# The first stage of a hybrid decoder layer: loads in quarters, three token tiles side by side, nine tiles on eight banks

## The chip, the cores and the metric

The kernel runs on one core of a Trainium2 chip, as one program. Its time is the device time of the whole program in microseconds (us); where several runs are shown, their median counts.

## The reference

The reference computes one layer of a hybrid decoder for two groups of requests: 1024 prompt tokens and 8 x 4 = 32 sample tokens of width 1024, all in fp32. Only the beginning of the layer is touched here. What matters of it:

```python
# u, v, cq, ckv, kpe: columns of one projection
u, v, cq, ckv, kpe = split_in(rms_norm(x, g_mix) @ w_in)    # widths 512, 512, 256, 256, 32

def chunk_gmlp(u, v, w_s, b_s, ln_g, ln_b):
    ...
    vg = layer_norm(gelu(v).reshape(n, t // c, c, 8, 64), ln_g, ln_b)
    w = where(tril(ones((c, c))), w_s[:, :c, :c], 0)
    mixed = einsum('gts,nmsgd->nmtgd', w, vg) + b_s[:, :c].T[:, :, None]
    return gelu(u) * mixed.reshape(n, t, 512), vg
```

Behind this come the latent attention over the prompt and over a paged cache, the output projection, attention into 256 memory tokens, and a gated convolutional FFN. They take most of the time and aren't changed.

## The kernel before

**Tiles.** The 1056 tokens are nine token tiles (`TILES`): eight of 128 (0 to 7, the prompt) and tile 8 of 32 (the samples). For the loads of x they are grouped into three chunks (`CH`) of 384, 384 and 288 tokens, so that a chunk covers three tiles. The 1024 features lie in eight blocks of 128 (k).

**Split products.** Each fp32 operand is written as a sum of two reduced-precision parts. `split` (L188) makes the high part on ACT (L192 a plain cast, L196 with a gain) and the low part on DVE (L193 or L199), and `mm3` (L180, matmul at L186) multiplies high by high, high by low and low by high. A tile of a projection, over eight blocks, is thus 24 matmuls into one PSUM bank. x is split once, into `xh` and `xl`, with the gain `g_mix` in it.

**The factor of the norm.** The RMS factor of a token is not put into x but applied afterwards: `rs_tok`, a scale for each token. `squares` (L315) has ACT square the token rows (L323, tiles `xt` for tokens 0 to 383 and space in `a_all` for the others) with a sum along the row, and DVE then makes the reciprocal root by some twelve small steps (`rsqrt`, L221 to L232). The gelu that reads a projection's bank (L426 for v, L456 for u) needs the `rs_tok` of its tile.

**Order of phase 1.** The columns of v and u come in two halves (`hf`), in this order: v0, u0, the gate products of half 0, v1, u1, the gate products of half 1. For each tile of v: 24 matmuls (`proj`, L342), the gelu (L426), and a LayerNorm over groups of 64 columns: sums on DVE (L427 to L432), squares on ACT (L431), the factor on DVE (L437), gain and bias on POOL (L439, L441). The result is split again into `vgh` (ACT) and `vgl` (DVE). The LayerNorm works on tiles 0 to 2, 3 to 5, 6 and 7, and 8 as groups. The gate products (`mm<-vgh,wsh`) need all eight tiles of `vgh` and `vgl`, and the matrices that `gate_matrices` (L370) makes; DVE takes them up at L467.

**Weights.** `wraw` loads a half's weights in two DMAs of four blocks, `wsplit` (L293) splits them in two steps of four blocks. There are two buffers each for raw and split weights.

**Banks.** The pool `ps1` has five PSUM banks named "mm", for all projections and gate products, and three named "st" for small sums.

**What sets the order.** Within phase 1 the SP queue, which issues the loads, follows the order in which the code is written until `loads.__exit__` (a manual schedule). Before the change that order is: v0's first half and x's chunk 0 first half, the same for the second halves, tokens of tile 0, chunk 1 in two halves, tokens of tiles 1 and 2, chunk 2, then tokens of tiles 3 to 6 (into `a_all`, in space that the loads of x free), the weights u0, the LayerNorm's rows, v1, and the matrices of the gate. The other engines' orders come from a scheduler that places instructions by its own estimates; a change in one place can reorder an engine elsewhere. Each engine then works its own list in order.

Of the kernel before, what the change touches and what calls it, by code (L numbers as in the profile page):

```python
# [5 lines left out]
F32 = mybir.dt.float32  # L6
# [7 lines left out]
P = 128  # L14
# [6 lines left out]
TILES = [(i * P, P) for i in range(8)] + [(NP_, NS)]  # L21
# [134 lines left out]
class Net:  # L156
# [122 lines left out]
    def phase1(self):  # L279
        nc, tc, I, O = self.nc, self.tc, self.I, self.O  # L280
        p = self.open("p1")
        pp = self.open("ps1", space=PSUM)
# [9 lines left out]

        def wsplit(name):  # L293
            raw = raws.pop(name)
            n = raw.shape[2]
            hi = self.t(p, [P, 8, 288], FR, "whi", 2)[:, :, :n]
            lo = self.t(p, [P, 8, 288], FR, "wlo", 2)[:, :, :n]
            for k in range(0, 8, 4):
                self.split(hi[:, k : k + 4], lo[:, k : k + 4], raw[:, k : k + 4])
            return hi, lo  # L300

        px = self.open("px")
        xts, xrs = [], []

        def xload(c, e):
            o, n = CH[c]
            xrs.append(self.t(px, [P, 4, 384], F32, "xr", 6)[:, :, :n])
            nc.sync.dma_start(xrs[-1], I["xT"][:, 4 * e : 4 * e + 4, o : o + n])

        def tload(i, place):  # L310
            t0, tn = TILES[i]
            xts.append(place[:tn])
            nc.sync.dma_start(xts[-1], I["x"][t0 : t0 + tn])

        def squares(p, i0, i1):  # L315
# [8 lines left out]
            self.rsqrt(p, self.rs_tok[:, i0:i1], ss, 1.0 / 1024)  # L324

        xt = lambda: self.t(px, [P, 1024], F32, "xt", 3)
        loads = tc.manual_schedule(engines={mybir.EngineType.SP})
        loads.__enter__()
        raws["v0"] = raw = self.t(pr, [P, 8, 288], F32, "wraw", 2)[:, :, :256]
        for e in range(2):  # L330
            k = slice(4 * e, 4 * e + 4)
            nc.sync.dma_start(raw[:, k], I["w_v0"][:, k])
            xload(0, e)
        tload(0, xt())
        for e in range(2):
            xload(1, e)
        tload(1, xt())
        tload(2, xt())
        for e in range(2):
            xload(2, e)  # L340
        w = wsplit("v0")
        for c, (o, n) in enumerate(CH):  # L342
            for k in range(8):
                self.split(xh[:, k, o : o + n], xl[:, k, o : o + n], xrs[2 * c + k // 4][:, k % 4], self.col("g_mix", k))
            if c == 0:
                squares(px, 0, 1)
            elif c == 1:
                squares(px, 1, 3)
        def proj(w, i, n):
            t0, tn = TILES[i]  # L350
            ps = self.t(pp, [P, 512], F32, "mm", 5)[:tn, :n]
            self.mm3(ps, [(xh[:, k, t0 : t0 + tn], xl[:, k, t0 : t0 + tn]) for k in range(8)],
                     [(w[0][:, k], w[1][:, k]) for k in range(8)])
            return ps
# [6 lines left out]
        for i in range(3, 7):  # L361
            tload(i, flat[:, (i - 3) * 1024 : (i - 2) * 1024])
        wraw("u0", I["w_u0"], 256)
        pg = self.open("pg")
# [37 lines left out]
        for hf in range(2):  # L402
# [8 lines left out]
            for i0, i1 in ((0, 3), (3, 6), (6, 8), (8, 9)):  # L411
# [9 lines left out]
                mu = self.t(pg, [P, 3, 4], F32, "mu", 2)[:tn, :m]  # L421
                rv = self.t(pg, [P, 3, 4], F32, "rv", 2)[:tn, :m]
                for i in range(i0, i1):
                    ps = proj(w, i, 256)
                    g, mi = gv[:, i - i0], mu[:, i - i0]
# [9 lines left out]
                for i in range(i0, i1):  # L435
# [1833 lines left out]
```

## Time and profile before

| quantity | value |
| --- | --- |
| median of 3 runs | 1914.36 us (1913.44 to 1916.24) |
| profiled execution | 1912.54 us |
| its span, first to last instruction | 1910.8 us |
| mean granted TensorE clock | 0.987 |
| PE busy | 1841.0 us (96%), 14338 matmuls |
| DVE busy | 1417.4 us (74%) |
| ACT busy | 929.5 us (49%) |
| POOL busy | 707.7 us (37%) |

The span is what the views of the trace divide; the 1.7 us between it and the execution's time lie around it. Times in the views are counted from the span's start. A row of a timeline has start, duration, engine, line, operation, output<-inputs, shapes and count, and in brackets the idle time before it and what released it. Matmuls overlap their successors, so the step from one start to the next, not the duration, tells the rate.

### The profile page before, as it was taken

To read this page: it belongs to the slowest core of one execution; us is meant where nothing else is said; L and a number is where in the kernel's file an instruction comes from. 1 tells how busy PE (TensorE), PEld (TensorE's weight loads), DVE (VectorE), ACT (ScalarE), POOL (GpSimd) and SP (SyncE) were. 2 spreads that over 40 slices of the span, in tenths; PEclk is the share of its full clock that TensorE was granted. 3 is DMA by queue.
4 is the path that set the end of the run, shared out by engine and by line. 5 is a ranking of instruction groups with operands and counts; after the bars stand their busy time and mean duration, and the time that the engine had idled before them with its cause. 6 is when DMAs were issued, how large, how long until landed. Compare 5 with 4: busy or idle time off the path is not lost.

```text
span 1910.8 us, 39909 instructions
## 1 busy us (share of the span) xinstructions
PE 1841.0 (96%) x14338; PEld 1724.7 (90%) x14338; DVE 1417.4 (74%) x3093; ACT 929.5 (49%) x1964; POOL 707.7 (37%) x816
## 2 busy tenths in 40 slices
PE   6999899999999999999899999999999999999999
PEld 6999777778989888989799988899999999999999
DVE  7865868776877677776754666688898888879664
ACT  6435676666555555555553355543333233345442
POOL 1221415643544454434313101057767667500000
PEclk9999899999999999999999999999999999999999
DMA  8102204656766655554564334422222322395242
GB/s 296 54 14 71 72 1 155 231 220 178 213 189 172 176 168 173 168 158 139 177 182 142 139 116 154 149 68 73 73 90 68 100 68 77 89 361 170 78 151 75
DMA packets 135704, 260.21 MB, mean 136 GB/s; under 512 B 20561, under 2 KB 78770, under 8 KB 132434
## 3 DMA queue, kind: packets, MB, share of 16 engines
q1 hardware_dynamic: 134642, 256.61, 42.8%
q8 instruction: 113, 1.85, 0.4%
q10 hardware_dynamic: 864, 1.05, 0.2%
q14 instruction: 85, 0.70, 0.1%
HBM read 212.30 MB, written 45.30 MB: 135 GB/s over the span
## 4 chain that ended last, share of the span: by engine, by line
PE 69%; DVE 9%; issue 5%; DMA 3%; POOL 2%; ACT 1%; SPq 0%; DVEq 0%; POOLq 0%; ACTq 0%
PE s L186 15%; PE d L186 12%; PE X L186 7%; PE b L186 7%; PE F L186 7%; PE E L186 6%; PE A L186 3%; PE y L186 2%; PE o L918 2%; PE tp L905 1%; PE o L1348 1%; DVE mx L1299 1%; POOL S L1296 1%; PE tp L860 1%; PE tp L186 1%
## 5 line engine op out<-in xcount | busy, mean ns | idle before, releaser
L186 PE MATMUL s<-w2h,ch 128*128 128x288 f32 (+1 forms) x1024 | 305.9, 299 | 0.0
L186 PE MATMUL s<-w2h,cl 128*128 128x288 f32 (+1 forms) x1024 | 295.1, 288 | 1.9 <-POOL cl L1235 1.9
L186 PE MATMUL s<-w2l,ch 128*128 128x288 f32 (+1 forms) x1024 | 294.6, 288 | 0.0
L186 PEld LDWEIGHTS s<-w2h,ch 128*128 128x128 f32 x1024 | 192.6, 188 | 19.1 <-issue 13.6
L186 PEld LDWEIGHTS s<-w2h,cl 128*128 128x128 f32 x1024 | 192.4, 188 | 2.4 <-POOL cl L1235 2.2
L186 PEld LDWEIGHTS s<-w2l,ch 128*128 128x128 f32 x1024 | 192.8, 188 | 0.0
L1278 DVE TENSOR_REDUCE ss<-sq 128x16 f32<-128x1024 f32 x128 | 155.4, 1214 | 47.8 <-ACT sq L1275 47.5
L1235 POOL TENSOR_TENSOR cl<-cT,ch 128x512 fp32r<-128x512 f32 x64 | 83.4, 1303 | 166.7 <-ACT ch L1231 154.3
L1275 ACT ACTIVATE sq<-s 128x512 f32<-128x512 f32 x128 | 76.5, 597 | 91.0 <-PE s L186 90.9
L1272 ACT ACTIVATE sq<-s 128x512 f32<-128x512 f32 x128 | 76.5, 598 | 82.1 <-PE s L186 81.7
L192 ACT CAST a<-brb 128x528 fp32r<-128x528 f32 x77 | 48.8, 634 | 110.7 <-PE d L186 107.3
L186 PE MATMUL mm<-whi,xh 128*128 128x256 f32 (+3 forms) x288 | 83.8, 292 | 16.1 <-ACT xh L196 9.9
L186 PE MATMUL d<-a,w 128*128 128x264 f32 x768 | 95.4, 284 | 1.2 <-DVE G L2048 1.2
L186 PEld LDWEIGHTS d<-a,w 128*128 128x128 f32 x768 | 94.3, 188 | 1.3 <-issue 1.3
L193 DVE TENSOR_TENSOR a<-brb,a 128x528 fp32r<-128x528 f32 x77 | 54.2, 705 | 55.5 <-ACT a L192 55.5
L186 PE MATMUL mm<-wlo,xh 128*128 128x256 f32 (+3 forms) x288 | 82.4, 289 | 0.0
L186 PE MATMUL mm<-whi,xl 128*128 128x256 f32 (+3 forms) x288 | 82.3, 290 | 0.0
L1925 POOL TENSOR_TENSOR lo<-s,hi 128x1024 fp32r<-128x1024 f32 x20 | 63.2, 3160 | 45.7 <-ACT hi L1924 45.7
L1974 ACT COPY a<-A 128x264 f32<-128x264 f32 x44 | 16.4, 374 | 122.4 <-PE A L186 114.4
L1231 ACT CAST ch<-cT 128x512 fp32r<-128x512 f32 x128 | 73.5, 628 | 3.6 <-DMA cT<-cT 3.5
L1274 DVE TENSOR_TENSOR S<-s,S 128x64 f32<-128x64 f32 x128 | 28.0, 219 | 60.8 <-ACT sq L1272 60.8
L186 PE MATMUL d<-a,hi 128*128 128x264 f32 x552 | 72.0, 284 | 0.0
(700 smaller groups left out, 6533.2 us busy)
## 6 DMA issues: line engine op xcount, KB each, us to landing
cT<-cT SPq DMA_DIRECT2D x256, 160.0 KB, 2.6
ck<-ck SPq DMA_DIRECT2D x256, 144.0 KB, 3.2
raw<-w_up SPq DMA_DIRECT2D x44, 512.0 KB, 3.6
wsumd<-wsum SPq DMA_DIRECT2D x13, 1024.0 KB, 3.8
actd<-cv SPq DMA_DIRECT2D x44, 264.0 KB, 2.5
brb<-actd SPq DMA_DIRECT2D x44, 264.0 KB, 6.2
wsum<-w_down SPq DMA_DIRECT2D x11, 1024.0 KB, 4.9
raw<-wsumd SPq DMA_DIRECT2D x20, 512.0 KB, 3.8
```

The lines of the kernel that those rows point to most:

```text
L186: self.nc.tensor.matmul(out, l, r, start=first and i == 0, stop=last and i == len(seq) - 1)
L192: {"act": nc.scalar.copy, "pool": nc.gpsimd.tensor_copy, "dve": nc.vector.tensor_copy}[eng](hi, src)
L193: low = lambda: nc.vector.tensor_tensor(lo, src, hi, ALU.subtract)
L860: nc.tensor.transpose(tp[:, j * P : j * P + P], s[x, g * 4 + j][:, h % 4], self.ident)
L918: nc.tensor.matmul(u["o"][jj * 64 : jj * 64 + 64, c], s["v"][:, j + jj, h % 4], th[:, jj * 256 : jj * 256 + c.stop - c.start], start=j == ...
L1231: nc.scalar.copy(d["h"][:, k], src[k])
L1235: (nc.vector if k else nc.gpsimd).tensor_tensor(d["l"][:, k], src[k], d["h"][:, k], ALU.subtract)
L1272: nc.scalar.activation(sq[:, 0], ps[:, :, n0 : n0 + 256], AF.Square)
L1274: nc.vector.tensor_tensor(S, ps[:, :, sc : sc + 32], S, ALU.add)
L1275: nc.scalar.activation(sq[:, 1], pt.rearrange("p (e d) -> p e d", e=2), AF.Square)
L1278: yield lambda: nc.vector.tensor_reduce(s["ss"][:, g0 : g0 + 2].rearrange("p e (z h) -> p z e h", z=2), sq.rearrange("p z e (h d) -> p z e ...
L1925: eng.tensor_tensor(lo, src, hi, ALU.subtract)
```

## The change

- The first weights (v0) and all of x come in quarters of two feature blocks instead of halves of four; x gets buffers of its own for each quarter. `wsplit` gets a step, two blocks for v0.
- Order of the loads: both first chunks of x come ahead of the first token rows, and the weights u0 are loaded directly behind the tokens of tiles 1 and 2, ahead of the tokens of tiles 3 to 6.
- The squares of tile 0 are written behind the split of chunk 1 and those of tiles 1 and 2 behind that of chunk 2, one chunk later each.
- The tiles of v0 are computed in threes: `first` runs over the feature blocks outside and over the three tiles of a chunk inside, each into a bank of its own. Tiles 5 to 7 use the three "st" banks, the others "mm".
- Six matmuls of a zero tile (f32, 128x256) are issued before all others, into tile 0's bank, as the opening of its accumulation.
- `gate_matrices` is called behind tile 8 instead of behind the first three tiles of half 0.

In the orders that result, PE has the six zero products, the 72 matmuls of tiles 0 to 2, those of 3 to 5, of 6 and 7, and tile 8; tile 8 takes the bank of tile 0, and tiles 0, 1 and 2 of u0 take those of tiles 1, 2 and 3. On ACT the two whi of u0 stand ahead of the gelus of tiles 0 to 2, and the two whi of u1 behind the last gelu of u0 and ahead of the last vgh. On DVE the two wlo of u0 stand among the rsqrt steps of tiles 1 and 2. On PE the gate products begin behind u0, and the first tile of v1 lies behind the first of them. POOL's order is the same. Later in the program only a few instructions trade places with neighbours.

```diff
-        def wsplit(name):
+        def wsplit(name, step=4):
...
-            for k in range(0, 8, 4):
-                self.split(hi[:, k : k + 4], lo[:, k : k + 4], raw[:, k : k + 4])
+            for k in range(0, 8, step):
+                self.split(hi[:, k : k + step], lo[:, k : k + step], raw[:, k : k + step])
...
-            xrs.append(self.t(px, [P, 4, 384], F32, "xr", 6)[:, :, :n])
-            nc.sync.dma_start(xrs[-1], I["xT"][:, 4 * e : 4 * e + 4, o : o + n])
+            xrs.append(self.t(px, [P, 2, 384], F32, f"xr{c}{e}")[:, :, :n])
+            nc.sync.dma_start(xrs[-1], I["xT"][:, 2 * e : 2 * e + 2, o : o + n])
...
+        zero = self.t(px, [P, 256], F32, "zero")
+        nc.vector.memset(zero, 0.0)
+        begin = self.t(pp, [P, 512], F32, "mm", 5)[:, :256]
+        for i in range(6):
+            nc.tensor.matmul(begin, zero[:, :P], zero, start=i == 0, stop=False)
...
-        for e in range(2):
-            k = slice(4 * e, 4 * e + 4)
+        for e in range(4):
+            k = slice(2 * e, 2 * e + 2)
             nc.sync.dma_start(raw[:, k], I["w_v0"][:, k])
             xload(0, e)
+        for e in range(4):
+            xload(1, e)
         tload(0, xt())
-        for e in range(2):
-            xload(1, e)
-        tload(1, xt())
-        tload(2, xt())
-        for e in range(2):
+        for e in range(4):
             xload(2, e)
-        w = wsplit("v0")
+        for i in range(1, 3):
+            tload(i, xt())
+        wraw("u0", I["w_u0"], 256)
+        w = wsplit("v0", 2)
         for c, (o, n) in enumerate(CH):
             for k in range(8):
-                self.split(..., xrs[2 * c + k // 4][:, k % 4], self.col("g_mix", k))
-            if c == 0:
+                self.split(..., xrs[4 * c + k // 2][:, k % 2], self.col("g_mix", k))
+            if c == 1:
                 squares(px, 0, 1)
-            elif c == 1:
+            elif c == 2:
                 squares(px, 1, 3)
+
+        def first(w, c):
+            ps = []
+            for i, (t0, tn) in list(enumerate(TILES))[3 * c : 3 * c + 3]:
+                ps.append((self.t(pp, [P, 512], F32, *(("st", 3) if 5 <= i < 8 else ("mm", 5))) if i else begin)[:tn, :256])
+            for k in range(8):
+                for (t0, tn), x in zip(TILES[3 * c :], ps):
+                    self.mm3(x, [(xh[:, k, t0 : t0 + tn], xl[:, k, t0 : t0 + tn])], [(w[0][:, k], w[1][:, k])],
+                             first=k == 0 and t0 > 0, last=k == 7)
+            return ps
...
-        wraw("u0", I["w_u0"], 256)
...
+                if hf == 0 and i0 % 3 == 0:
+                    firsts = first(w, i0 // 3)
                 for i in range(i0, i1):
-                    ps = proj(w, i, 256)
+                    ps = proj(w, i, 256) if hf else firsts[i % 3]
...
-                if hf == 0 and i0 == 0:
+                if hf == 0 and i0 == 8:
                     gate_matrices()
```

More of the change, by code (lines that the diff above doesn't have):

```diff
@@ L329, in phase1 @@
         raws["v0"] = raw = self.t(pr, [P, 8, 288], F32, "wraw", 2)[:, :, :256]
-        for e in range(2):
-            k = slice(4 * e, 4 * e + 4)
+        for e in range(4):
+            k = slice(2 * e, 2 * e + 2)
             nc.sync.dma_start(raw[:, k], I["w_v0"][:, k])
             xload(0, e)
+        for e in range(4):
+            xload(1, e)
         tload(0, xt())
-        for e in range(2):
-            xload(1, e)
-        tload(1, xt())
-        tload(2, xt())
-        for e in range(2):
+        for e in range(4):
             xload(2, e)
-        w = wsplit("v0")
+        for i in range(1, 3):
+            tload(i, xt())
+        wraw("u0", I["w_u0"], 256)
+        w = wsplit("v0", 2)
         for c, (o, n) in enumerate(CH):
             for k in range(8):
-                self.split(xh[:, k, o : o + n], xl[:, k, o : o + n], xrs[2 * c + k // 4][:, k % 4], self.col("g_mix", k))
-            if c == 0:
+                self.split(xh[:, k, o : o + n], xl[:, k, o : o + n], xrs[4 * c + k // 2][:, k % 2], self.col("g_mix", k))
+            if c == 1:
                 squares(px, 0, 1)
-            elif c == 1:
+            elif c == 2:
                 squares(px, 1, 3)
+        def first(w, c):
[7 more added lines that the diff above has]
+            return ps
         def proj(w, i, n):
```

## The prediction

> **What bounds the kernel now.** I read the page's head and slices first, then the waits of the first 120 us, the busy time by stage, and the timelines of ACT, DVE, POOL, PE and SP over that stretch, which is nearly all that the change touches.
>
> ```profile
> span 1910.8 us, 39909 instructions
> PE   6999899999999999999899999999999999999999
> PE 69%; DVE 9%; issue 5%; DMA 3%; POOL 2%; ACT 1%; SPq 0%; DVEq 0%; POOLq 0%; ACTq 0%
> ```
>
> PE works nearly everywhere and carries 69% of the chain that ends last. Only its slice 0 (47.8 us) has room that this change can reach. The profiled execution took 1912.54 us, 1.7 us more than its span. The median of the runs is 1914.36, 1.8 above the profiled one, so a gain worked out from the trace is taken off the median. A difference of 0.2%, 3.8 us, is about the least that this kernel's measurement tells from none.
>
> ```profile
> PE mm L186 <- ACT gv L426: 6.2, 1, 6.2
> ...
> PE mm L186 <- ACT xh L196: 9.9, 1, 9.9
> ```
> ```profile
> 10.00:30.00 20.00, 19.95 (x151) 19.75 (x152) 18.06 (x60) 16.80 (x34) 0.00 (x0) 1.00 0.74 261
> ...
> 35.00:41.00 6.00, 0.08 (x1) 0.00 (x0) 5.58 (x21) 3.31 (x5) 1.47 (x2) 0.75 1.04 364
> 41.00:45.00 4.00, 3.69 (x19) 2.98 (x20) 3.71 (x10) 2.79 (x8) 4.00 (x6) 0.53 1.07 356
> 45.00:60.00 15.00, 15.00 (x129) 14.80 (x127) 14.75 (x53) 9.57 (x20) 6.07 (x8) 1.00 0.48 164
> 60.00:70.00 10.00, 10.00 (x87) 9.91 (x86) 8.21 (x36) 3.53 (x9) 3.85 (x6) 1.00 0.00 1
> ...
> 80.00:100.00 20.00, 20.00 (x174) 19.81 (x173) 15.29 (x58) 6.78 (x17) 4.64 (x6) 1.00 0.13 44
> ```
>
> The columns are the stretch, the busy time of PE, PEld, DVE, ACT and POOL, the granted clock, the DMA share and GB/s. PE has two holes: 9.9 us until the first split of x, and 6.2 us from 35 to 41, after which it has half clock (0.53) until about 45. From there it is full. DVE is as full from 45 to 60 (14.75 of 15), which will matter below.
>
> ```profile
> 41.31 0.42 PE L186 MATMUL mm<-whi,xh 128*32 128x256 f32 x1 [6.23 <-ACT gv L426]
> ...
> 44.73 0.30 PE L186 MATMUL mm<-wlo,xh 128*32 128x256 f32 x1
> ```
> ```profile
> 40.78 1.20 ACT L426 ACTIVATE gv<-mm,rs_tok 128x256 f32<-128x256 f32 x3 [1.95 <-DVE rs_tok L232]
> ```
> ```profile
> 27.47 0.41 DVE L427 TENSOR_REDUCE mu<-gv 128x4 f32<-128x256 f32 x1
> ...
> 40.01 0.68 DVE L232 SCALAR_TENSOR_TENSOR rs_tok<-rqa,rqy 128x3 f32<-128x3 f32 x1
> ```
>
> In the second hole PE wants to begin token tile 8 (the form 128*32) of v0, and has no bank until the gelu of tile 3 has read one. That gelu waits for rs_tok of tiles 3 to 5, the end of a chain of loads, squares (ACT) and rsqrt steps (DVE). The hole's end is set by that chain and not by PE's work. So for each edit I ask what it does to this chain, and what PE can do meanwhile.
>
> **Quarters and zero products: nothing by themselves.**
>
> ```profile
> GB/s 0 118 196 257 357 383 367 400 379 371 386 410 385 388 266 32 0 5 46 295 385 407 396 317 407 350 367 364 378 326 333 403 178 24 208 373 110 0 0 11
> ```
> ```profile
> 9.19 2.13 ACT L196 ACTIVATE xh<-xr,cols 128x384 fp32r<-128x384 f32 x4 [1.81 <-DMA xr<-xT]
> ...
> 16.10 4.24 ACT L196 ACTIVATE xh<-xr,cols 128x384 fp32r<-128x384 f32 x8 [0.21 <-DMA xr<-xT]
> 20.25 1.04 ACT L323 ACTIVATE xt<-xt 128x1024 f32<-128x1024 f32 x1
> ...
> 22.33 3.51 ACT L196 ACTIVATE xh<-xr,cols 128x288 fp32r<-128x288 f32 x8
> ```
> ```profile
> 9.85 0.58 PE L186 MATMUL mm<-whi,xh 128*128 128x256 f32 x1 [9.85 <-ACT xh L196]
> 10.23 0.42 PE L186 MATMUL mm<-wlo,xh 128*128 128x256 f32 x1
> 10.45 0.41 PE L186 MATMUL mm<-whi,xh 128*128 128x256 f32 x1
> ```
> ```profile
> 0.82 0.39 SPq L245 DMA_DIRECT2D cols<-cols  x1
> ```
> ```profile
> L918 PE MATMUL o<-pth,v 128*64 128x256 f32 x256 | 52.0, 405 | 0.8 <-ACT pth L907 0.6
> ```
>
> The GB/s row shows 0 to 60 us in slices of 1.5. Summed, it reaches the first halves of w and x with the small columns (1.38 MB) at 7.5 us; the first xh starts at 9.19, 1.7 later. The first quarters are 0.73 MB, reached at 5.4: xh starts at about 7.1 and PE at 7.7 instead of 9.85. The six zero products are plain f32, a form that this stretch does not show. The low end is the cold step of a split product, 0.21 us (10.23 to 10.45); the high end is twice the 0.405 of the nearest plain form (L918), 0.81, for the half clock. That is 1.3 to 4.9 us; I take the high end, since L918 is nearer in kind. Begun by 1.5 us, as SP's first load is at 0.82, they end by 6.4, ahead of 7.7, and delay nothing. Were they longer than 6.2 us, PE would start later by the rest, and the slack of 3.1 us found below covers that. An earlier first product also pays nothing, while the second hole stands.
>
> **The chain of rs_tok: unchanged to 0.3 us.**
>
> ```profile
> 36.29 1.04 ACT L192 CAST whi<-wraw 128x1024 fp32r<-128x1024 f32 x1 [0.29 <-DMA wraw<-w_u]
> 37.79 1.05 ACT L192 CAST whi<-wraw 128x1024 fp32r<-128x1024 f32 x1 [0.45 <-DMA wraw<-w_u]
> ```
> ```profile
> 37.37 1.22 DVE L193 TENSOR_TENSOR wlo<-wraw,whi 128x1024 fp32r<-128x1024 f32 x1
> ...
> 38.86 1.22 DVE L193 TENSOR_TENSOR wlo<-wraw,whi 128x1024 fp32r<-128x1024 f32 x1
> ```
> ```profile
> 27.12 1.76 SPq L313 DMA_DIRECT2D a_all<-x  x4
> 28.93 1.22 SPq L291 DMA_DIRECT2D wraw<-w_u  x2
> ```
>
> On SP the two loads of u0 go ahead of the token rows a_all, with the first tokens' load behind x's second chunk. The splits of u0 stand in the new order ahead of the gelus of tiles 0 to 2 on ACT, and inside the rsqrt chain of tiles 1 and 2 on DVE. The load of x's second chunk completes 4.2 MB, reached in the GB/s row at 15.0, used from 16.7; its last two xh (4.24/8 each) end at 17.8. Then ACT has a square (1.04), eight xh (3.51), two squares (2.08): 24.4; and the two whi of u0 (2.1): 26.5. All that and u0 is 8.1 MB: 7.0 are there at 22.5, and 1.05 more at 385 GB/s make 25.2, used from 26.9, so the last whi ends between 26.5 and 28.0. DVE's second wlo follows 1.22 later, and a few rsqrt steps: rs_tok of tiles 1 and 2 at about 30.2, where the LayerNorm of the first tiles begins at 27.47 now. That is 2.7 later. But from 27.47 to the end of rs_tok (40.69) DVE now also does the two wlo of u0, 2.4, which are done then. So gelu of tile 3 comes at 40.78 + 2.7 - 2.4 = 41.1. If ACT and not DVE sets this part, the 2.4 isn't won back: 43.5. If the loads come a little sooner, 40. I take 41.1, by DVE's row (5.58 busy of 6.0).
>
> **More banks and side by side: 8.4 us of PE's work ahead of the hole.**
>
> ```profile
> 68.93 0.28 PE L186 MATMUL mm<-whi,xh 128*32 128x256 f32 x1
> ...
> 71.73 0.39 PE L186 MATMUL mm<-vgh,wsh 128*128 128x512 f32 x1
> ```
>
> A tile of 24 products takes 71.73 - 68.93 = 2.80 us. Now eight lie ahead of the hole. With three banks of "st" beside the five, tile 8 needs only the gelu of tile 0, and tiles 0 and 1 of u0 those of tiles 1 and 2, all due by 31; tile 2 of u0 is the first that needs the gelu of tile 3. So 11 tiles lie ahead: 7.7 + 30.8 = 38.5, then a hole of 3.1 until 41.6. Behind it 7 tiles of u0 are left, not 10: 41.6 + 19.6 = 61.2, where u0 ends at 71.73 now. That is 10.5 us earlier.
>
> **What is late next: the LayerNorm of v0.**
>
> ```profile
> 66.65 0.40 ACT L192 CAST vgh<-gv 128x256 fp32r<-128x256 f32 x1
> ...
> 72.30 2.19 ACT L192 CAST whi<-wraw 128x1152 fp32r<-128x1152 f32 x2
> 78.21 0.47 ACT L426 ACTIVATE gv<-mm,rs_tok 128x256 f32<-128x256 f32 x1 [3.71 <-PE mm L186]
> ```
>
> Behind u0 PE's queue holds the gate's products (vgh), with the first tile of v1 behind them. They need the last vgh, done at 67.05 now, 26.3 us after the gelu of tile 3. In between DVE is full, and the change takes nothing from its work there: vgh comes at 41.1 + 26.3 = 67.4. The whi of u1 (2.19) moves ahead of it on ACT, at about 61.7 to 64, and hides in that wait. So PE has a new hole, 61.2 to 67.4, and its gate products start 71.73 - 67.4 = 4.3 us earlier. Of the 10.5, 6.2 are given back. Such a hole has its price: after the one of 6.23, 16 products took from 41.31 to 44.73, 3.4 us in place of 1.9 (16 of 2.80/24): 1.5 lost. I charge it, as this hole is as long: 4.3 - 1.5 = 2.8. Behind it PE is full again (20.00 of 20 from 80 to 100), with DVE at 15.29, so I let the 2.8 pass to the end. The price may be 0 or, with a longer half clock, 3: the gain is 1.3 to 4.3.
>
> [...]
>
> **Rivals.** *PE bound throughout*: the LayerNorm gets ready by 62, because DVE and POOL are less in each other's way once u0's split and the gate matrices lie elsewhere. For it: gate_matrices moves behind the last tiles. Against it: DVE's 14.75 of 15. It gives 8 to 10.5: 1904 to 1906.
>
> *Gain lost on ACT*: the 2.4 isn't won back, the gelu comes at 43.5, vgh at 69.8: 4.3 - 2.4 - 1.5 = 0.4, 1914.0. For it: ACT carries two whi more ahead of its first gelus.
>
> *Slower by late loads*: u0's splits now stand in order ahead of the first gelus, on ACT and DVE, so a late u0 moves the whole chain one for one. If 21 smaller loads kept to the pace of the early slices (196 to 257, mean 226 GB/s), 8.1 MB would take 35.8 and be used from 37.5, 10.6 us after 26.9: 2.8 - 10.6 = -7.8, 1922.2. It ends slower than now by 0.2% from a use at 33.5 on. Against it: from 6 us on the row keeps to 357 to 410, with loads of 512 KB in it, twice the new quarters of w.
>
> ```profile
> wraw<-w_v SPq DMA_DIRECT2D x4, 512.0 KB, 7.7
> ```
>
> [...]
>
> **How the numbers follow.** Forecast 0.60, 1914.36 - 2.8 = 1911.6. PE bound 0.12, lost on ACT 0.16, late loads 0.12. Of the forecast's own 1910.1 to 1913.1, spread by 1 us for the chain's walk, somewhat under half lies beyond 3.8: 0.28. Faster: 0.28 + 0.12 = 0.40; same 0.32 + 0.16 = 0.48; slower 0.12. The range, 1905.5 to 1915.5, leaves out the late loads and the best part of the PE-bound case.
>
> **What would show it.** Right: first split product near 7.7; PE idle about 38.5 to 41.6, ended by the gelu of tile 3; a second hole from 61 to 67 ended by vgh, with half clock behind it; gelu of v1's first tile near 75.4 (78.21 now). Wrong: no second hole (PE bound); rs_tok of tiles 3 to 5 beyond 43; the last xh of x's second chunk behind 20, or u0's whi behind 30 (late loads).

## The result, and the profile after

The changed kernel is slower: median 1921.92 us (nine runs, 1917.98 to 1928.06) beside 1913.01 of the kernel before (nine runs, 1909.23 to 1916.24), ratio 1.0045 with a 95% interval of 1.0034 to 1.0056. The forecast was 1911.6, with a range up to 1915.5. The profiled execution took 1928.06 us, the longest of the nine; a second profile of the same kernel, further below, took 1921.01. What both show is told apart from what only one shows.

Head and PE slices of the page after:

```profile
span 1926.3 us, 39955 instructions
...
PE   8999899998999999999899999899999999999999
```

Slice 0 went from 6 to 8, so the edit fills PE where it was meant to. But slices 9 and 25 (from 433 and from 1204 us) show an 8 now where the kernel before has a 9: in this profile something is lost far behind the edited stretch too.

Waits of the first 120 us after (engine, what it waited for, total us, times, longest):

```profile
ACT gv L447 <- DVE rs_tok L232: 6.9, 2, 5.2
...
PE mm L186 <- ACT gv L447: 5.4, 1, 5.4
PEld mm L186 <- ACT vgh L192: 4.5, 1, 4.5
```

Busy time by stage after, in the columns of the prediction:

```profile
35.00:41.00 6.00, 4.37 (x37) 4.17 (x36) 5.61 (x27) 3.95 (x7) 2.27 (x3) 1.00 0.97 288
41.00:45.00 4.00, 0.27 (x1) 0.28 (x2) 3.86 (x6) 0.80 (x3) 3.94 (x6) 0.87 0.65 257
45.00:60.00 15.00, 15.00 (x107) 14.85 (x108) 11.67 (x50) 9.62 (x23) 0.37 (x1) 0.81 0.23 71
60.00:70.00 10.00, 7.81 (x67) 7.31 (x66) 9.37 (x25) 4.64 (x10) 6.39 (x9) 1.00 0.00 1
70.00:80.00 10.00, 8.00 (x33) 7.29 (x34) 8.48 (x23) 1.89 (x5) 1.43 (x2) 0.66 0.35 107
```

PE after:

```profile
1.26 5.38 PE L332 MATMUL mm<-zero 128*128 128x256 f32 x12 [1.26 <-DVE zero L329]
7.66 0.39 PE L186 MATMUL mm<-whi,xh 128*128 128x256 f32 x1 [1.02 <-ACT xh L196]
...
44.73 0.58 PE L186 MATMUL mm<-whi,xh 128*128 128x256 f32 x1 [5.36 <-ACT gv L447]
...
72.00 2.07 PE L186 MATMUL mm<-vgh,wsh 128*128 128x512 f32 x4 [4.19 <-ACT vgh L192]
```

ACT after (gelu of tile 3, last vgh of half 0, first gelu of v1):

```profile
44.20 0.84 ACT L447 ACTIVATE gv<-mm,rs_tok 128x256 f32<-128x256 f32 x2 [5.25 <-DVE rs_tok L232]
...
71.25 0.69 ACT L192 CAST vgh<-gv 128x256 fp32r<-128x256 f32 x2
...
80.71 0.48 ACT L447 ACTIVATE gv<-mm,rs_tok 128x256 f32<-128x256 f32 x1 [4.78 <-PE mm L186]
```

Both holes are where the prediction put them, ended by what it named, but each ends late. The first gelu of v1 is 2.5 us later than before, where 2.8 sooner were forecast. In the second profile of the changed kernel the same three rows come a little earlier, and its first gelu of v1 is 1.1 later than before:

```profile
43.78 0.84 ACT L447 ACTIVATE gv<-mm,rs_tok 128x256 f32<-128x256 f32 x2 [5.26 <-DVE rs_tok L232]
...
70.22 0.69 ACT L192 CAST vgh<-gv 128x256 fp32r<-128x256 f32 x2
...
79.35 0.48 ACT L447 ACTIVATE gv<-mm,rs_tok 128x256 f32<-128x256 f32 x1 [4.43 <-PE mm L186]
```

**Why the gelu of tile 3 is late.** DVE after, from the LayerNorm's factor for tiles 0 to 2 to rs_tok of tiles 3 to 5, and the one wait that follows:

```profile
38.07 0.16 DVE L232 SCALAR_TENSOR_TENSOR rqy<-rqa,rqy 128x3 f32<-128x3 f32 x1
38.17 1.63 DVE L458 TENSOR_TENSOR gv<-gv,rv 128x256 f32<-128x256 f32 x3
39.72 0.68 DVE L229 TENSOR_TENSOR rqa<-rqy 128x3 f32<-128x3 f32 x1
40.44 0.65 DVE L230 TENSOR_TENSOR rqa<-rqa,rqh 128x3 f32<-128x3 f32 x1
41.12 0.65 DVE L232 SCALAR_TENSOR_TENSOR rqy<-rqa,rqy 128x3 f32<-128x3 f32 x1
...
43.16 1.01 DVE L232 SCALAR_TENSOR_TENSOR rs_tok<-rqa,rqy 128x3 f32<-128x3 f32 x1
...
54.93 0.15 DVE L408 COPY bs_s<-st 32x8 f32<-32x8 f32 x1 [2.13 <-PE st L406]
```

The same steps before:

```profile
36.87 0.15 DVE L229 TENSOR_TENSOR rqa<-rqy 128x3 f32<-128x3 f32 x1
37.06 0.16 DVE L230 TENSOR_TENSOR rqa<-rqa,rqh 128x3 f32<-128x3 f32 x1
```

POOL after, then POOL before, each at its first LayerNorm work, and SP's load of the LayerNorm's rows, after and before:

```profile
38.73 2.33 POOL L460 TENSOR_TENSOR gv<-gv,rows 128x256 f32<-128x256 f32 x3 [37.72 <-DVE gv L458]
41.02 2.08 POOL L462 TENSOR_TENSOR gv<-gv,rows 128x256 f32<-128x256 f32 x3
```
```profile
39.53 2.52 POOL L439 TENSOR_TENSOR gv<-gv,rows 128x256 f32<-128x256 f32 x3 [38.51 <-DMA rows<-rows]
```
```profile
23.69 0.33 SPq L385 DMA_DIRECT2D rows<-rows  x1
```
```profile
30.19 1.26 SPq L366 DMA_DIRECT2D rows<-rows  x1
```

A step on three numbers for each partition takes 0.65 us, not 0.16, while POOL does the gain and bias. POOL's own instructions take 2.08/3 = 0.69 there, and the steps follow each other every 0.68 to 0.72: DVE gets in about one step for each instruction of POOL. Before, POOL waited for the LayerNorm's rows until 39.53, when five of these six steps were done. After, SP issues the rows at 23.69 instead of 30.19, and POOL starts as soon as DVE has given it data. That is only 0.80 us sooner (38.73), while the first of the steps comes 2.85 us later (39.72 instead of 36.87): both together put the steps beside POOL, and how much each is worth in this order is not shown. The price already stands in a row that the prediction shows: the last step before, at 40.01, is the one of the six that ran beside POOL, and it took 0.68. In a version told below, `b_first`, POOL began only at 40.81, and the same step took 0.15. What makes the step that slow beside POOL, the traces do not show; they show 0.65 to 1.01 beside it and 0.15 to 0.16 without it.

**Behind the first 120 us.** The start of the same ACT instruction, changed kernel minus kernel before (us), near the named time of the kernel before. The third to fifth columns are runs told below.

| time | after | after, again | `a_st35` | `a_u0late2` |
| --- | --- | --- | --- | --- |
| 78 (first gelu of v1) | +2.5 | +1.1 | -0.9 | -2.3 |
| 120 | +3.2 | +2.2 | -0.5 | -2.3 |
| 185 | +3.3 | +2.3 | -0.4 | -2.2 |
| 245 to 260 | +4.5 | +7.3 | +0.4 | -0.1 |
| 425 to 445 | +3.3 | +6.1 | -0.8 | -1.1 |
| 545 to 570 | +6.2 | +7.1 | -0.8 | -1.2 |
| 665 to 690 | +9.1 | +8.4 | +0.2 | -1.2 |
| 1152 to 1177 | +9.6 | +7.3 | -0.2 | -4.3 |
| 1366 to 1395 | +12.7 | +7.8 | +1.1 | -2.7 |
| 1825 to 1854 | +15.5 | +8.5 | +1.9 | -0.4 |

The two profiles of the changed kernel agree on a loss of 2 to 3 us in the first 120 and on one of 1 to 3 between 560 and 680. Around 222 the second loses 5.0 by 258, of which 3.8 are left at 445; the first loses 1.2, and nothing of it is left at 445. The rest comes in one profile and not in the other.

### The profile page after: what moved, and what is told of

Same layout as the page of the kernel before. It is cut to its first block, busy times and chain, and to the rows that moved or that the text cites. A ratio compares the mean times of both kernels' runs of the same rounds, so it can differ in the third digit from the quotient of the medians.

```text
span 1926.3 us, 39955 instructions
## 1 busy us (share of the span) xinstructions
PE 1857.6 (96%) x14350; PEld 1740.5 (90%) x14350; DVE 1418.8 (74%) x3096; ACT 930.1 (48%) x1966; POOL 707.2 (37%) x816
## 3 DMA queue, kind: packets, MB, share of 16 engines
q10 hardware_dynamic: 864, 1.05, 0.2%
## 4 chain that ended last, share of the span: by engine, by line
PE 75%; DVE 10%; DMA 6%; issue 4%; ACT 2%; POOL 2%; SPq 1%; DVEq 0%; POOLq 0%; ACTq 0%
PE s L186 16%; PE d L186 12%; PE b L186 8%; PE mm L186 7%; PE X L186 6%; PE F L186 6%; PE E L186 6%; PE A L186 3%; PE o L939 2%; PE tp L926 1%; DMA yd<-res 1%; PE o L1369 1%; PE tp L881 1%; DVE mx L1320 1%; DVE rqa L229 1%
## 5 line engine op out<-in xcount | busy, mean ns | idle before, releaser
L186 PE MATMUL mm<-whi,xh 128*128 128x256 f32 (+3 forms) x264 | 76.9, 295 | 6.4 <-ACT gv L447 5.4
L186 PE MATMUL mm<-wlo,xh 128*128 128x256 f32 (+3 forms) x264 | 75.9, 290 | 0.0
L186 PE MATMUL mm<-whi,xl 128*128 128x256 f32 (+3 forms) x264 | 74.5, 294 | 0.0
```

Of the source, the lines that this page charges most:

```text
L186: self.nc.tensor.matmul(out, l, r, start=first and i == 0, stop=last and i == len(seq) - 1)
```

## The experiments

All ratios are to runs of the kernel before on the same chip, in brackets the 95% interval.

**Both kernels again, nothing changed.**

> The kernel before, unchanged, for a second trace. The theory that the part of the loss behind the first 110 us is a matter of half-clock spells that short PE holes set off by chance expects the first 200 us to repeat within 0.5 us, and the spells behind 200 us to come at other holes than in the first trace (steps of 1 to 3.5 us against it, in both directions), with a time of 1909 to 1916. The rival, that a kernel's spells belong to its order of instructions, expects the same spells at the same holes.

1913.72, ratio 1.0003 (0.9989 to 1.0017). The second trace repeats the first to 0.5 us until 190 us; behind that the difference of the two lies between +1.1 and +2.5.

> The changed kernel, unchanged, for a second trace. Both theories expect the first 110 us to repeat: gelu of tile 3 near 44.2, gelu of v1's first tile near 80.7, 2.5 to 3.5 us behind the kernel before at 110 us. If the spells at 467, 631, 921, 1262 and 1696 us are chance, most of them are absent or at other holes here, and the time is 1918 to 1924; if they belong to the changed order of later instructions, they stand at the same holes again, some 6 us or more of loss behind 200 us.

1920.52, ratio 1.0034 (1.0021 to 1.0047). Busy time by stage of the first profile of the changed kernel, then of the second:

```profile
460.00:480.00 20.00, 16.85 (x123) 16.64 (x122) 11.89 (x29) 10.62 (x23) 7.91 (x13) 0.91 0.66 192
...
620.00:640.00 20.00, 17.92 (x139) 16.16 (x138) 16.94 (x36) 9.21 (x21) 9.12 (x16) 0.91 0.54 156
...
1690.00:1710.00 20.00, 17.50 (x132) 17.31 (x131) 12.37 (x20) 8.18 (x15) 0.00 (x0) 0.91 0.97 343
```
```profile
460.00:480.00 20.00, 17.81 (x140) 17.39 (x139) 14.91 (x32) 12.24 (x27) 7.95 (x14) 1.00 0.68 190
...
620.00:640.00 20.00, 17.92 (x151) 16.16 (x151) 17.73 (x37) 9.84 (x22) 10.64 (x17) 1.00 0.52 145
...
1690.00:1710.00 20.00, 19.30 (x158) 19.33 (x159) 11.52 (x18) 8.08 (x14) 0.00 (x0) 1.00 1.00 355
```

From 620 to 640 PE is idle for the same 2.08 us in both, yet the granted clock is 0.91 in one and 1.00 in the other. Whether half clock follows this hole differs from run to run of one program. The two profiles of the one kernel ended 7.0 us apart. So a profile's end time says little here, and only what recurs is explained below.

**One part undone.** The zero products left out (`a_nozero`: the memset and the six matmuls gone, `first` from the first product on):

> The changed kernel without the six zero products. Theory: they end by 6.7 us, ahead of the first split product, and beyond keeping the clock full from 6.4 us on they move nothing: the first split product stays at 7.6 to 7.8, the second hole keeps its end (gelu of tile 3 near 44.2), and the time at 110 us is within 0.5 us of the changed kernel. [...]

1919.85, ratio 1.0034 (1.0018 to 1.0050): as slow as the whole change. The gelu of tile 3 comes at 43.57, the first gelu of v1 at 78.80. That is near the second profile of the whole change (43.78 and 79.35), so the profiles do not tell the two apart; by the median, the zeros aren't the cause.

The load of u0 back where it was (`a_u0late`):

```diff
-        wraw("u0", I["w_u0"], 256)          # behind the tokens of tiles 1 and 2
...
         for i in range(3, 7):
             tload(i, flat[:, (i - 3) * 1024 : (i - 2) * 1024])
+        wraw("u0", I["w_u0"], 256)
```

> The changed kernel with the load of u0 back behind the tokens of tiles 3 to 6. The low parts of u0 (2 x 1.22) then stand again between the last rsqrt steps of tiles 3 to 5, and the first LayerNorm begins 2.4 us sooner. Theory (the steps beside POOL are what cost): LayerNorm of tiles 0 to 2 from 28 to 28.5, POOL's first work from 36 or so, beside both the wlo and the steps; gelu of tile 3 at 41 to 43, at least 1 us before the changed kernel's 44.2. In this build the two transposes that the change moved at about 222 us stand as in the kernel before, so the hole of 3.65 there should be 2.0 again and the time at 285 us within 2 us of the kernel before. In all 1914 to 1918. Rival (all of the loss is in the first 110 us): the loss at 285 us stays what it is at 110.

1911.01, ratio 0.9984 (0.9968 to 1.0000). PE, ACT and DVE of this version:

```profile
39.90 0.58 PE L186 MATMUL mm<-wlo,xh 128*128 128x256 f32 x1 [3.33 <-DVE wlo L193]
...
68.53 1.21 PE L186 MATMUL mm<-vgh,wsh 128*128 128x512 f32 x4 [1.25 <-ACT vgh L192]
```
```profile
43.34 0.84 ACT L447 ACTIVATE gv<-mm,rs_tok 128x256 f32<-128x256 f32 x2 [6.51 <-DVE rs_tok L232]
...
75.72 0.47 ACT L447 ACTIVATE gv<-mm,rs_tok 128x256 f32<-128x256 f32 x1 [4.77 <-PE mm L186]
```
```profile
52.95 0.15 DVE L408 COPY bs_s<-st 32x8 f32<-32x8 f32 x1
```

This was the lowest median so far, with an interval that touches 1, so it was run again (`a_u0late2`):

> The changed kernel with the load of u0 back behind the tokens 3 to 6, a second time. If the early load of u0 is what costs, its gain repeats: first gelu of v1 at 75.5 to 76.5 (78.21 in the kernel before), ratio 0.997 to 0.999. If 0.9984 was chance: 1.000 to 1.002.

1911.76, ratio 0.9989 (0.9973 to 1.0004), first gelu of v1 at 75.90. The 22 runs of both against the 47 beside them give 0.9989 with 0.9980 to 0.9997 (ratio of the means, two standard errors): about 0.1% faster than the kernel before, and 9 to 11 us faster than the whole change. The gain over the kernel before is weakly shown: the second set alone reaches 1.0004, the version was repeated because it was low, and `b_quarters` below is as low (0.9988).

It is instructive that the gelu of tile 3 is as late here, 43.34, with POOL beside the rsqrt steps too. What differs is what follows. DVE takes bs_s without a wait, the last vgh is done at 68.48, 25.1 us after the gelu (27.7 in the changed kernel, 71.94 - 44.20), and PE's second hole shrinks to 1.25, with no half clock behind it (1.00 granted from 60 to 80). That the wait for bs_s makes the difference is only in part shown: in the versions with the changed kernel's order of phase 1, the stretch is 26.7 with a wait of 0.96 (`a_nozero`), 27.1 with 1.52 (`a_again`) and 27.7 with 2.13, but 27.5 with 3.24 (`a_ident`, told below). The waits for u0's own parts (2.39 for whi, 3.33 for wlo) are the price, and they lie where PE would have stood anyway.

The gate's matrices back behind the first three tiles (`a_gate0`, `i0 == 8` to `i0 == 0`):

> The changed kernel with gate_matrices back behind the first three tiles. Theory: gelu of tile 3 stays near 44.2, since POOL still works beside the rsqrt steps; but DVE's wait for the gate's small products (2.1 us, within the LayerNorm of tiles 3 to 5) comes earlier or goes, so that the last vgh is 1 to 3 us sooner than 71.9. In this build, too, the two transposes at 222 us stand as before: the hole of 3.65 is 2.0 and the loss at 285 us is no more than at 110 us. In all 1914 to 1918. Rival: the gate's work is the same wherever it is, last vgh within 0.5 us of 71.9, 1919 to 1922.

1927.93, ratio 1.0071 (1.0045 to 1.0098): worse still, the opposite of the expectation. PE and ACT of this version:

```profile
29.21 0.42 PE L186 MATMUL mm<-whi,xh 128*32 128x256 f32 x1 [7.22 <-ACT gv L447]
```
```profile
56.27 0.47 ACT L447 ACTIVATE gv<-st,rs_tok 128x256 f32<-128x256 f32 x1 [2.80 <-PE st L186]
```

The gate's small sums and tiles 5 to 7 now want the same three banks. The tiles are put off (their gelus wait for PE until 56.27), and PE comes to tile 8 at 22.0 and stands for 7.22. Moving `gate_matrices` is thus needed for the three extra banks.

**One part alone, on the kernel before.** The quarters and `step=2`, in the old order of loads (`b_quarters`):

> The kernel before with only the loads and splits of v0 and x in quarters; order of loads, banks and u0 as before. Theory: the first split product comes near 7.7 to 8 us in place of 9.85, and nothing else moves: the second hole still ends with the gelu of tile 3 near 40.8 (0.5 either way), so it is only longer; time within 1 us of the kernel before. Rival: ten more loads delay the later ones by 1 us or more, and the gelu comes at 42 or later.

1912.11, ratio 0.9988 (0.9974 to 1.0001); first gelu of v1 at 78.25 (78.21). The quarters cost nothing and pay nothing that is told from none.

The load of u0 alone, moved ahead (`b_u0soon`):

> The kernel before with only the load of u0 moved ahead of the tokens of tiles 3 to 6. Theory: the low parts of u0 go into the rsqrt chain of tiles 1 and 2, the LayerNorm of tiles 0 to 2 begins 2 to 3 us later than 27.47, and the last rsqrt steps of tiles 3 to 5 run beside POOL at 0.65 us in place of 0.16: gelu of tile 3 at 43 to 44.5 in place of 40.8, hole in PE 2 to 3.5 us longer, and the time 2 to 5 us slower. Rival: u0's 2.4 us on DVE are won back, gelu of tile 3 at 41 or earlier, time within 1 us.

1914.19, ratio 1.0004 (0.9991 to 1.0017). POOL and ACT of this version:

```profile
37.61 2.35 POOL L439 TENSOR_TENSOR gv<-gv,rows 128x256 f32<-128x256 f32 x3 [36.60 <-DVE gv L437]
```
```profile
43.16 1.20 ACT L426 ACTIVATE gv<-mm,rs_tok 128x256 f32<-128x256 f32 x3 [6.28 <-DVE rs_tok L232]
...
81.17 0.47 ACT L426 ACTIVATE gv<-mm,rs_tok 128x256 f32<-128x256 f32 x1 [3.71 <-PE mm L186]
```

The mechanism is there without any other part: POOL starts at once, the six steps take 0.65 to 1.01 each, the gelu of tile 3 is 2.4 late and v1's first gelu 3.0. But the median moves by only 0.4, with an interval that reaches to 3.3: in the profile the delay stays, in the median it can't be told.

The side-by-side tiles and banks alone (`b_first`):

> The kernel before with only the banks and the side-by-side order (tiles 0 to 2 together, tiles 5 to 7 in st); loads in halves, u0 late, no zero products. Theory: gelu of tile 3 stays near 40.8; PE has 11 tiles ahead of it, the hole is shorter than 6.2 (from about 40 on, since PE starts at 9.85), u0 ends at 61 to 63 in place of 71.7, and PE then waits for the last vgh near 67, so v1's first gelu is 2 to 4 us ahead of the kernel before (78.2). The two transposes at 222 us are moved here too, with their ACT casts: no larger hole there. In all 2 us faster to 2 slower. Rival: banks and order cost by themselves; v1's first gelu at 79 or later.

1917.65, ratio 1.0025 (1.0012 to 1.0038), slower against the expectation: PE stands 8.18 us until u0's first whi at 37.81, tiles 6 and 7 wait for their banks as in the version above (gate matrices are early here), and v1's first gelu is at 82.27.

**POOL.** Gain and bias of tiles 0 to 2 of half 0 left to the split alone, so that this work of POOL is not beside the steps (`a_nopool`):

```diff
+                    if hf == 0 and i < 3:
+                        self.split(vgh[:, i], vgl[:, i], gf)
+                        continue
```

> The changed kernel without POOL's gain and bias for token tiles 0 to 2 of half 0 (left out; the split reads the product before them). Theory: DVE's rsqrt steps for rs_tok of tiles 3 to 5 take 0.65 to 0.68 us in place of 0.16 because POOL works beside them (38.7 to 43.1). Without POOL's work there they take 0.16 to 0.17, rs_tok ends about 3 us sooner, and the gelu of tile 3 comes at 41.0 to 41.6 in place of 44.2; the whole is faster than the changed kernel by 3 us or more at 110 us. Rival: the squares on ACT and not the steps on DVE set it; then the gelu stays at 43.5 or later.

1915.81, ratio 1.0008 (0.9994 to 1.0023). DVE and ACT of this version:

```profile
39.41 0.15 DVE L229 TENSOR_TENSOR rqa<-rqy 128x3 f32<-128x3 f32 x1
39.81 0.16 DVE L230 TENSOR_TENSOR rqa<-rqa,rqh 128x3 f32<-128x3 f32 x1
```
```profile
42.18 0.84 ACT L447 ACTIVATE gv<-mm,rs_tok 128x256 f32<-128x256 f32 x2 [1.25 <-DVE rs_tok L232]
```

Five of the six steps take 0.15 to 0.16 again; the fourth, at 40.75, takes 1.00, beside POOL's work on the gate's matrices (L393, 1.10 from 40.64). That is the direct proof of what slows them. The gelu comes 2.0 sooner than in the first profile (1.6 than in the second), not the full 2.6 to 3.2 expected, because three vgl got in between the steps and one step still takes 1.00. The first gelu of v1, at 78.50, gains 2.2 on the first profile and 0.9 on the second, and at 120 us this version is 1.8 and 0.8 ahead of the two, not the 3 expected. The median falls by some 5, more than that: in this version the hole near 222 is 1.41, and the one near 628 is 1.06 as before.

The LayerNorm's rows loaded behind v1 and the identity, so that POOL should wait as before (`a_rows`):

> The changed kernel with the LayerNorm's rows loaded behind v1 and the identity. Theory: in the kernel before POOL could not begin before 38.5 us because the rows came late, and that kept it away from DVE's last rsqrt steps; the changed kernel has the rows early. With the rows later POOL begins 1 to 3 us later, fewer steps take 0.65, and the gelu of tile 3 comes at 41 to 43 in place of 44.2. The build also has the two transposes at 222 us where the kernel before has them, so no loss there. Time 1911 to 1916. Rival: the rows still land before 38 us, or the steps are not what sets the gelu: 44 and 1915 to 1918.

1917.97, ratio 1.0027 (1.0014 to 1.0040). The rows still landed in time: POOL starts at 38.48 all the same, one wlo of v1 gets between the steps, and the gelu of tile 3 comes at 46.07. A miss: with early u0, what the rows' load is worth stays untested.

Both moves, late u0 and late rows (`a_u0late_rows`):

> Both: u0's load back behind the tokens of tiles 3 to 6, and the rows behind v1 and the identity. Theory: POOL begins at 38 or later instead of 35.7, the wlo of u0 and the last rsqrt steps run at their own pace, the gelu of tile 3 comes at 40 to 41 in place of 43.3 and v1's first gelu at 72 to 74 (75.7 with u0 late alone, 78.2 before). Time 1907 to 1910, faster than the kernel before by 0.2 to 0.35%. Rival: the wait only moves to u0's weights or to the gate's vgh, and the time is that of u0 late alone, 1911.

1913.19, ratio 0.9993 (0.9980 to 1.0005). Here the late rows do act: POOL starts at 37.34 (35.68 with late u0 alone), behind the first three steps, which take 0.15 to 0.16, and three are left at 0.65 to 0.68. The gelu of tile 3 comes at 41.25 now, 2.1 sooner than with late u0 alone, yet v1's first gelu at 76.39 is 0.7 later: u0 ends sooner, a second hole of 2.12 opens ahead of the gate products, and half clock follows (from 69.9 to 72.0 the gate products come every 0.42 to 0.43, with late u0 alone, from 70.3 on, every 0.23 to 0.24). A sooner gelu is worth nothing when the LayerNorm behind it isn't sooner as well (last vgh at 67.8 against 68.5).

**The hole near 222 us.** PE there, in the kernel before, in the changed one, and in the version with other banks told last:

```profile
221.00 0.83 PE L860 MATMUL tp<-ident,k 128*96 128x128 f32 x6 [2.04 <-issue]
```
```profile
225.46 1.49 PE L881 MATMUL tp<-ident,k 128*96 128x128 f32 x6 [3.67 <-ACT hsq L832]
```
```profile
221.52 0.40 PE L881 MATMUL tp<-ident,k 128*96 128x128 f32 x2 [1.42 <-issue]
```

In the changed kernel the first transposes of the attention part wait for ACT's squares; before, the profile names nothing that they wait for. In the built program of the changed kernel their bank is the one that the last squares read; before, it is one that was read earlier. First guess: ACT's order beside PE's. The loads of v1 and the identity swapped, which moves ACT's cast of kTh (`a_ident`):

> The changed kernel with the loads of v1 and of the identity in the other order. In the changed kernel the attention's opening at about 222 us has PE's last two transposes of k behind two more groups of scores, while ACT's cast of them stands ahead of its first exponential, so ACT waits for PE there; in this build that cast stands behind the first exponential. Theory (this mismatch of orders is the 4 us that the changed kernel loses between 200 and 285 us in two of three traces): first 110 us as in the changed kernel within 1 us (loss 2 to 3.5), no further loss at 285 us, time 1915.5 to 1918. Rival (the loss there is chance or follows from phase 1): 1919 to 1923, with a loss of 5 to 7 us at 285.

1923.61, ratio 1.0060 (1.0043 to 1.0078), the hole still 3.67. That guess fell.

One spare tile of the transposes' pool taken ahead of them, to shift the banks by one (`a_rot`):

```diff
+            if x == "k" and g == 0 and h == 0 and not hasattr(self, "spare"):
+                self.spare = self.t(pp, [P, 512], F32, "tp", 4)[:96]
+                nc.tensor.matmul(self.spare[:96, :1], self.ones[:, :96], self.ones[:, :1], start=True, stop=True)
```

> The changed kernel with one spare PSUM tile (a product of one column) taken from the attention's banks just ahead of its first transposes, so that these get the next bank of the rotation. In the changed kernel they get the bank that ACT's last squares of the stage read last, and PE waits 3.66 us at 222 us; here they wait only for POOL's rope of k. Theory (the rotation of banks, shifted by another order in phase 1, costs 1.6 us and what half clock adds): the hole is under 2.1 us, the loss against the kernel before at 430 us is no more than at 180 us (2 to 3.5), and the time is 1916 to 1919, 2 to 4 us below the changed kernel. Rival (the hole is hidden in a stage that waits for other things anyway): time as the changed kernel, 1920 to 1922.

1920.69, ratio 1.0032 (1.0022 to 1.0042). The spare product itself now waits 3.62 for the squares; the hole only changed its owner. The same on the kernel before, three spares (`b_rot3`) and one (`b_rot1`), and on the version with late u0 (`a_u0late_rot`):

> The kernel before with three such spare tiles, so that its first transposes get the bank that ACT's last squares read, as in the changed kernel. Theory: a hole of about 3.7 us at 220 us in place of 2.05, and a time 1.5 to 4 us longer than the kernel before, 1915.5 to 1918. Rival: within 1 us of the kernel before.

1916.93, ratio 1.0013 (0.9998 to 1.0028); the spares wait 2.01 for the squares and the transposes another 0.99 behind them, 3.0 in all. That is short of the case it was to make, and the median can't be told from that of the kernel before.

> The kernel before with one spare tile: its first transposes wait only for POOL. Theory: the hole of 2.05 us at 219 us goes down to under 1.5, time 0 to 2 us below the kernel before. The three spare products themselves cost nothing that is seen (PE waits there), which this run checks for the other two. Rival: the chain behind (casts of k, DVE) is late anyway and the time is the same within 1 us.

1915.15, ratio 1.0009 (0.9996 to 1.0022), the hole 2.01.

> The changed kernel with u0's load back behind the tokens of tiles 3 to 6 and one spare tile ahead of the first transposes. Theory: v1's first gelu at 75.7 as with u0 late alone (78.2 before), so 2.4 us ahead at 110 us, and no loss at 222 us: 1909 to 1911.5, faster than the kernel before by 0.1 to 0.25%. Rival: the 2.4 us are used up behind 110 us, and the time is within 1 us of the kernel before.

1912.73, ratio 0.9998 (0.9987 to 1.0009), the hole 2.92. These four decide nothing. What shifts the hole is a change of banks far ahead of it (`a_st35`):

```diff
-                ... (("st", 3) if 5 <= i < 8 else ("mm", 5)) ...
+                ... (("st", 3) if 3 <= i < 6 else ("mm", 5)) ...
```

> The changed kernel with the three extra banks given to tiles 3 to 5 instead of 5 to 7; nothing else differs. In its built order the first transposes of the attention part follow, in their bank, a tile that was read earlier, not the one that ACT's last squares read. Theory A (which bank they get makes the hole near 222 us): the hole is 2.1 us or shorter, as in the kernel before (2.04 to 2.06), not 3.65, and the offset against the kernel before does not grow from 200 to 258 us, where it grew by 3 to 4 in the two profiles of the changed kernel. Theory B (the hole is set by ACT, which arrives late whatever the bank): 3.6 again. Both: the first 120 us stay as in the changed kernel, gelu of tile 3 at 43.5 to 44.5, first gelu of v1 at 79 to 81. Median by A 1917 to 1919, by B 1920 to 1921.

1914.92, ratio 1.0007 (0.9994 to 1.0020). The hole of 3.67 is gone (1.42 is left), and the offset goes only from -0.4 to +0.4 across it. So a change in which banks the first tiles take reaches this hole, 150 us later. It is not alone in that: with tiles 5 to 7 left in "st", the hole is also 1.41 with POOL silent (`a_nopool`), 2.06 with late rows (`a_rows`) and 2.77 with late u0 (`a_u0late`). Its price in time, 0 to 4 us by the table above, is not isolated: the first 120 us changed too, against the expectation. With tiles 6 and 7 holding "mm" banks, PE stands once for 7.94 (until 48.80) instead of 5.36 and 4.19, there is no second hole (10.00 busy of 10 from 60 to 70), and v1's first gelu comes at 77.35, with the gelu of tile 3 as late as ever, 44.15.

**The hole near 628 us.** PE there, before and after:

```profile
622.98 0.29 PE L1326 MATMUL m<-ident,mx 128*32 128x128 f32 x1 [1.06 <-DVE mx L1323]
```
```profile
630.19 0.28 PE L1347 MATMUL m<-ident,mx 128*32 128x128 f32 x1 [2.08 <-DVE mx L1344]
```

The same product waits 1.0 longer for DVE in both profiles of the changed kernel and in `a_nozero`, `a_ident`, `a_rot` and `a_st35`: 2.04 to 2.08 in all. In the fourteen other traces it waits 1.05 to 1.08, with late u0 and in `a_rows` too. The six profiles with the longer hole lose 0.9 to 2.9 us between 570 and 690 us against the kernel before, the others at most 0.1. Three of the six have a granted clock of 0.91 from 620 to 640 and lose 2.6 to 2.9 (the first profile, `a_ident`, `a_rot`); the other three have 1.00 and lose 0.9 to 1.3. What makes the hole longer was not tried.

## Why the prediction was wrong, point by point

- **Quarters and zeros: right.** The zeros end at 6.6 (6.4 forecast), the first split product starts at 7.66 (7.7). From 7.88 on the split products come every 0.11 to 0.12, where the kernel before has 0.21 to 0.22 until 13.86. Neither pays, nor costs (`b_quarters`, `a_nozero`). The case of late loads is out: u0's last whi ends at 29.0 (26.5 to 28.0 forecast), not behind 30. The added loads are eight (v0's go from two to four, x's from six to twelve), not the ten that the expectation of `b_quarters` names, and `b_quarters`, with 0.9988, shows no price for them.
- **Tiles ahead of the first hole: right.** 11 tiles, hole from 39.4 (38.5).
- **The chain of rs_tok: wrong, the step that failed first.** The LayerNorm of tiles 0 to 2 begins at 30.82 (30.2), and the two wlo were out of the way as forecast. But gelu of tile 3 came at 44.20, not 41.1: 3.1 late. The sum took the 0.16 of the rows before for steps that would now run beside POOL. The prediction let the LayerNorm begin 2.7 later and rs_tok end 0.3 later, and did not ask what would then run beside the last steps, though its own row at 40.01 has the one step beside POOL at 0.68. POOL's start moved too, by 0.8, as the rows' issue came at 23.69 and not 30.19. That is not the work of u0's move alone: the issue is at 25.47 with the quarters alone, 28.99 with u0's move alone, and 23.02 in `a_u0late`, where u0 is back.
- **26.3 us from that gelu to the last vgh: too short by 1.4.** "In between DVE is full" did not hold: 11.67 of 15 from 45 to 60. DVE stood 2.13 for bs_s, whose small products lie on PE's queue behind u0 tiles, which ran at half clock after the first hole (0.50 granted from 45 to 49, 0.81 from 45 to 60). `a_u0late` has no such wait, and needs 25.1; that the whole 1.4 is this wait is argued, not shown, as told with that version. The second profile needs 27.1.
- **Half clock 1.5: too small.** From the start of the gate products to v1's first gelu it takes 80.71 - 72.00 = 8.71, before 78.21 - 71.73 = 6.48: 2.2 lost. But the two stretches do not hold the same work: before, eight small products of the gate (74.54 to 75.10, 0.56) lie ahead of that gelu, and in the changed kernel they lie behind it, at 86.73. So the loss is nearer 2.8, and the 0.56 are part of why +2.5 at 78 us is +3.2 at 120. There were two holes with half clock behind them (0.81 granted from 45 to 60, 0.66 from 70 to 80), and only one was charged. The prediction's 0 and 3 for that price were the author's estimates; the trace after shows the 2.8.
- **The sum.** 75.4 + 3.1 + 1.4 + 0.7, and 0.1 from vgh to the product, is 80.7 (0.7 being 2.2 less the 1.5 charged): the first gelu of v1 as measured. In the second profile the gelu of tile 3 is 2.7 late, the stretch to vgh 0.8 too short, and v1's first gelu comes at 79.35.
- **"I let the 2.8 pass to the end": wrong.** That step saw no hole between 80 us and the end that the edit could touch. A change of the first tiles' banks reaches the transposes at 222 us, and a further hole of 2.08 near 628 came with it.
- **The rivals.** "Gain lost on ACT" had the right time for the gelu (43.5) for the wrong reason: ACT waited 5.25 for DVE. "PE bound" failed at both holes. The chance of 0.12 for a slower kernel hung on late loads alone, which did not come. No rival held the mechanism above.

What the whole comes to: in the two profiles phase 1 gives +2 to +3 instead of -2.8, the hole at 222 us 0 to +4, that at 628 us +1 to +3; the median is 7 to 9 above the kernel before. The late gelu alone does not cost that: `a_st35` (44.15) and `a_u0late` (43.34) have it about as late and are not told to be slower than the kernel before, and u0's early load alone brings it (43.16) for a median 0.4 higher. Late u0, other banks and a silent POOL, three edits of different kinds, each take most of the loss away; so no single part carries it. Four things stay open: how the parts act together; what makes the hole near 628; the separate price of the one at 222; and how much of the 7 to 9 us is that there are more and longer holes, each with its chance of half clock (three of six profiles at the hole of 2.04 to 2.08).

## What to carry to other kernels

When a step is moved, price its neighbours with what will run beside them, not with what ran beside them before: here the steps came 2.85 us later and POOL 0.80 us sooner, and DVE's smallest steps went from 0.16 to 0.65 us. A row of the kernel before that stands out (0.68 among steps of 0.16) is worth asking why. Follow the load order behind the moved load, and look for longer waits far behind the edit. Before explaining the end of a single profile, take a second one of the same kernel: two differed here by 7 us, as much as the effect.

## What was not expected of the hardware

DVE's rsqrt steps, on as little as three numbers a partition, take nearly as long as the instruction that POOL runs beside them: 0.64 to 0.69 against POOL's 0.69 for gain and bias, 1.01 for the last of them in the changed kernel against POOL's 1.09 (L393, from 43.06), and 0.15 to 0.17 with POOL silent. With late u0 the last takes 1.05, up to the end of POOL's 2.15 (L393, from 41.08).

Half clock followed a hole far shorter than the 6.2 us that the prediction went by: 0.91 granted from 620 to 640 after a hole of 2.08, and 1.00 after the same hole in the next profile. In all it followed this hole in three of six profiles, and the hole of 1.05 to 1.08 at the same place in none of fourteen. What decides between the two is not shown.
